# Transposed projections in three 256-column products a step, summed in half a PSUM bank

## The chip, the cores and the metric

The kernel runs on one core of a Trainium2 chip. The metric is the time of one execution on the device, in microseconds (us). TensorE multiplies (PE in the profile; PEld is its load of the stationary operand), VectorE (DVE) and ScalarE (ACT) work on elements, GpSimd (POOL) issues a few transfers, and SyncE (SP) issues the large ones. Products are summed in PSUM, in banks of 512 float32 columns.

## What is computed

Two transformer layers over 256 tokens of width 2048, in float32. Layer 0 has attention with forget gates, layer 1 has sparse attention over keys and values made from layer 0's output. Each layer ends with a squared-Relu MLP of width 8192, and each half of a layer with a layer norm.

```python
def sq_relu_mlp(x, w1, w2):
    return jnp.square(jax.nn.relu(x @ w1)) @ w2
...
    for layer in range(DEPTH):
        if layer < N_A_LAYERS:
            mix = fox_attention(h, fox_w_in[layer], fox_b_f[layer], fox_w_o[layer])
        else:
            b = layer - N_A_LAYERS
            mix = nsa_attention(h, nsa_w_in[b], nsa_w_o[b], rel_bias, *kv)
        h = layer_norm(ALPHA * h + mix, ln1_g[layer], ln1_b[layer])
        h = layer_norm(ALPHA * h + sq_relu_mlp(h, mlp_w1[layer], mlp_w2[layer]), ln2_g[layer], ln2_b[layer])
        if layer == N_A_LAYERS - 1:
            kv = shared_kv(h, kv_w, cmp_pos_k, cmp_pos_v, cmp_k_w1, cmp_k_w2, cmp_v_w1, cmp_v_w2)
```

## The kernel before

Every float32 operand of a large product is held as two parts of type float32r, a high part and a low rest (`fill_split`, L117 on ScalarE for the high part and L118 on VectorE for the rest). A product x @ W is then the sum of three: high by high, high by low, low by high.

Weights come in blocks of 128 partitions x 1024 columns (512 KB), loaded by SyncE's queue into `raw` (4 buffers) and split into `whl` (5 buffers, [128, 2, 1024]: high, low). Activations lie transposed in chunks `act` of [128, 4, 2, 256]: four blocks of 128 features, and for each the high parts of the 256 tokens and, right behind them, the low ones, so that one block gives a contiguous moving operand of 512 columns.

There are two kinds of large product:

- `xs_part` and `xs_mm` (L173) have activations as the stationary operand and 512 columns of weights as the moving one; three 512-column products a step, the first two with the same stationary block. They make values, the output projections and the second matrix of the MLP. The change leaves them alone.
- `ws_many` (L141 to L156) has 128 columns of a matrix, a slice, as the stationary operand and activations as the moving one, so that the product comes out transposed: [128 columns of W, 256 tokens]. A slice is two blocks of weights and 16 steps. A step is a wide product (L151): high weights by the 512 columns of high and low activations, into a whole bank `acc`; and a low product (L152): low weights by the 256 high activations, into the first half of the bank. In the last step the low product comes ahead of the wide one. After 16 steps the two halves of the bank have to be added.

`merge` (L182 to L189) does that: ScalarE copies the second half to SBUF (L185), VectorE adds it to the first half (L187, or L189 with a scale). `ws_many` and `merge` serve the queries and keys of layer 0 (`project`, 32 slices), the hidden layer of both MLPs (`use` in `mlp`, 128 slices; VectorE's L385 then does the squared Relu and `fill_split` fills the next chunk), the transposed keys and values (`use_raw` and `use_k`, 16 slices) and the queries of layer 1 (16 slices). In the attentions the logits, transposes and weighted sums of earlier heads are put between the slices (`at` and `run`). A scheduler sets the order on each engine from the program's order and its own estimates.

In `ws_many` before:

```python
            for w, acc in zip(ws, accs):
                wide = lambda: mm(acc, w[:, 0, s], a, start=kt == 0, stop=last)
                low = lambda: mm(acc[:, :S], w[:, 1, s], a[:, 0, :], start=False, stop=False)
                if last:
                    low(), wide()
                else:
                    wide(), low()
```

Of the kernel before, what the change touches and what calls it, by code (L numbers as in the profile page):

```python
# [19 lines left out]
P = 128  # L20
# [3 lines left out]
G = 4  # L24
# [28 lines left out]
def constants():  # L53
    """Identity, triangles, stacked identities and masks: they depend on shapes alone."""
    i = np.arange(P)
    eye = np.eye(P, dtype=np.float32)
    upper = (i[:, None] <= i[None, :]).astype(np.float32)
    causal = np.where(i[None, :] > i[:, None], np.float32(BIG), np.float32(0))

    def stacked(n):  # L60
        a = np.zeros((P, n), np.float32)
        a[np.arange(2 * n), np.arange(2 * n) % n] = 1
        return a

    t = np.arange(S).reshape(2, P)
    d_c = t[:, :, None] - (16 * np.arange(NC) + 31)
    keep = (d_c >= 0).astype(np.float32).transpose(1, 0, 2).reshape(P, 2 * NC)
    cst = [eye, upper, np.ones((P, P), np.float32), np.zeros((P, P), np.float32), causal,
           stacked(60), stacked(48), stacked(16), keep]

    def onehot(*dists):
        """Block k of 32 rows picks the bucket of distance k; row 96 + k says that the key lies ahead."""
        a = np.zeros((99, len(dists[0])), np.float32)
        c = np.arange(len(dists[0]))
        for k, dist in enumerate(dists):
            ok = dist >= 0
            a[NB * k + buckets(dist)[ok], c[ok]] = -1
            a[96 + k, c[~ok]] = 1
        return a

    oh = [onehot(255 - np.arange(384))]
    for tb in range(2):
        oh += [onehot(*(d_c[tb, :, n + k] for k in range(3))) for n in range(0, NC, 3)]
    ahead = np.zeros((99, 3, H), np.float32)
    ahead[[96, 97, 98], [0, 1, 2]] = BIG
    oh.append(ahead.reshape(99, 3 * H))
    return np.ascontiguousarray(np.concatenate(cst, 1)), np.ascontiguousarray(np.concatenate(oh, 1))
# [11 lines left out]
def _trunk(nc, tc, i, out, ctx):  # L99
# [23 lines left out]
    def wload(src, k, pool=wp, bufs=5, pieces=1):  # L123
        """Half k of a block of weights, split."""
        raw = raw_tile()
# [16 lines left out]
    def ws_many(srcs, acts, accs, half=None):  # L142
        """accs = (128 columns of a matrix each)^T @ x^T, over the wide halves of x; half: rows 0-1023 or the rest."""
        for kt in range(KT) if half is None else range(8 * half, 8 * half + 8):
            if kt % 8 == 0:
                ws = [wload(src, kt // 8) for src in srcs]
            a = acts[kt // 4][:, kt % 4]
            s = slice(kt % 8 * P, (kt % 8 + 1) * P)
            last = kt == KT - 1
            for w, acc in zip(ws, accs):  # L150
                wide = lambda: mm(acc, w[:, 0, s], a, start=kt == 0, stop=last)  # L151
                low = lambda: mm(acc[:, :S], w[:, 1, s], a[:, 0, :], start=False, stop=False)  # L152
                if last:
                    low(), wide()
                else:
                    wide(), low()  # L156

    def ws_stream(srcs, acts, use, together=1):
        """Each of srcs is one 128-column slice of a matrix; use(j, acc) gets its product, transposed."""
        j = 0  # L160
# [14 lines left out]
    def xs_part(src, act, accs, first, last, pieces=1):  # L175
        """accs[t] += (512 columns of x)[tokens t] @ 512 x 512 of a matrix"""
        ws = [wload(src, k, pieces=pieces if k == 0 else 1) for k in range(2)]
# [3 lines left out]

    def merge(dst, acc, scale=1.0):  # L182
        """dst = scale * (the wide product's two halves)"""
        t = sp.tile([P, S], F32, tag="mt", name="mt")
        nc.scalar.activation(t, acc[:, S:], AF.Copy, scale=scale)  # L185
        if scale == 1.0:
            nc.vector.tensor_add(dst, acc[:, :S], t)  # L187
        else:
            nc.vector.scalar_tensor_tensor(dst, acc[:, :S], scale, t, op0=OP.mult, op1=OP.add)  # L189

    def narrow(src, n, acts, st, dst):
        """dst[:, tok, :] = x @ (2048 x n) for a small n; returns its last step."""
        raw = wp.tile([P, KT, n], F32, tag="raw", name="nraw", bufs=4)
# [32 lines left out]
    def out_proj(src, acts, first, ln=None, two=False, between=()):  # L226
        """h = (ALPHA h or h) + acts @ W, 512 columns at a time (two: the first 1024 at once).

        between's steps come after the parts. With ln, the last 512 columns are left to what it returns,
        which ends with the layer norm."""  # L230
        between = list(between)
# [36 lines left out]
        def end(late, meanwhile=None):  # L268
            """Tokens 128-255 come behind, so that the norm of the others overlaps with their products."""
            ln.gains(late)  # L270
# [30 lines left out]
    class Norm:  # L301
        """Layer norm of h in place, in pieces of 128 tokens x 512 features, with what use does to a piece."""

# [55 lines left out]
    def transposer(cs):  # L359
        """Puts the pieces into cs, transposed and split, in chunks of 512 features."""  # L360
        def use(t, c):
# [14 lines left out]
    def mlp(layer, acts, ln):  # L376
        for q in range(4):
            hid = []

            def use(j, acc):  # L380
                if j % 4 == 0:
                    hid.append(act_chunk())
                u = sp.tile([P, S], F32, tag="mu", name="mu")
                merge(u, acc)
                nc.vector.scalar_tensor_tensor(u, u, 0.0, u, op0=OP.max, op1=OP.mult)  # L385
                fill_split(hid[-1][:, j % 4, 0, :], hid[-1][:, j % 4, 1, :], u)
# [5 lines left out]

    # ---- attention: the steps that both kinds share
    def exp_rows(E, L, m, sums):
# [4 lines left out]

    # ================= layer 0: forgetting attention  # L400
    bfb = cp.tile([P, H], F32, name="bfb")
# [8 lines left out]
    def warm(n, lhs, rhs):  # L410
        """Keeps the tensor engine's clock up while it waits."""
        idle = ps_lg.tile([P, 512], F32, tag="lg", name="idle")
# [18 lines left out]
    def forget_gates():  # L431
        """Log of the forget gates."""
        f = sp.tile([P, 5, 2, H], F32, name="f", bufs=1)
# [29 lines left out]
    with tc.tile_pool(name="fp", bufs=2) as fp:  # L463
# [16 lines left out]
        def project(name, hd, sc):  # L480
            acc = acc_tile()
            ws_many([i[name][hd]], xs, [acc])
            x = fp.tile([P, S], F32, tag=name, name=name)
            merge(x, acc, sc)
            return x
# [92 lines left out]
    with tc.tile_pool(name="late", bufs=2) as late:  # L578
# [6 lines left out]
        def tables():  # L585
            """Tables of the relative bias, negated, with BIG where a key lies ahead"""
            r_ps = ps_lg.tile([P, 512], F32, tag="lg", name="rps")
# [17 lines left out]

    # ================= layer 1: sparse attention over keys and values of layer 0's output
    with tc.tile_pool(name="np", bufs=2) as np_:
# [4 lines left out]
        gate = np_.tile([P, 2, 3 * H], F32, name="gate", bufs=1)  # L612
        # keys of the two branches and of the compressed blocks, split: per group, high and low parts of
        # [selected 0-127, window 0-127, compressed, selected 128-255, window 128-255]
        kT = np_.tile([P, G, 2, KW], F32R, name="kT", bufs=1)
        kcT = np_.tile([P, G, NC], F32, name="kcT", bufs=1)
        vhl = np_.tile([P, 2, 2, 512], F32R, name="vhl", bufs=1)
        v1 = np_.tile([P, 2, 512], F32, name="v1", bufs=1)
        # compressed values in three bands of rows (high, high, low parts), to meet high, low and high weights
        vc = np_.tile([BAND, G, P], F32R, name="vc", bufs=1)  # L620
# [5 lines left out]
        def bands(t):  # L626
            """The three bands of the columns of t"""
            return bass.AP(tensor=t.tensor, offset=t.offset, ap=[*[list(x) for x in t.ap[:-1]], [32, 3], [1, NC]])
# [3 lines left out]
        def use_raw(j, acc):  # L632
            merge(raws[:, j // G, j % G, :], acc)

# [20 lines left out]
        def use_k(j, acc):  # L655
            x = np_.tile([P, S], F32, tag="q", name="k")
            merge(x, acc)
            s, g = j // G, j % G
# [16 lines left out]
        def compress(s):  # L675
            """First product of the compression; returns its later steps."""
            acc = acc_tile()
# [158 lines left out]
        for hd in range(H):  # L836
# [7 lines left out]
            qT = np_.tile([P, S], F32, tag="q", name="q")  # L844
            merge(qT, acc, -SCALE)
            at(n + 2, scores(hd, qT, bm))
# [11 lines left out]
def laid_out(a):  # L858
    """The inputs in the order in which the kernel reads them."""
    def cols(w):  # L860
        # 128 columns of all rows, in two halves of the rows: [n, half, p, (kt c)]
        k, n = w.shape
        return w.reshape(2, k // P // 2, P, n // P, P).transpose(3, 0, 2, 1, 4).reshape(n // P, 2, P, HALF)

    def rows(w):
        # 512 columns of 512 rows, in two halves of the rows: [n, kc, half, p, (kt c)]
        k, n = w.shape
# [53 lines left out]
```

## Time and profile before

| what | value |
|---|---|
| median of the runs | 2260.76 us (2259.89 to 2261.65, 3 runs) |
| span of the profiled execution, first to last instruction | 2258.3 us |
| mean granted TensorE clock in it | 0.995 of full speed |
| TensorE's matmuls busy | 2233.2 us (99%) |
| VectorE busy | 1406.5 us (62%) |
| ScalarE busy | 1047.0 us (46%) |
| products of L151, L152 and L173 | 3072, 3072 and 4416 |

The page gives the busy time of an engine as the union of its instructions; matmuls overlap in it, since the next starts streaming before the last has drained. The time line gives starts, and the distance from one start to the next is what a product takes from the engine. The chain of waits goes back from the last instruction to what released it, step by step, and shows what the end of the kernel hung on.

### The profile page before, as it was taken

How to read it: one execution, taken by the hardware profiler on the slowest of the kernel's cores; microseconds unless marked ns; L12 is line 12 of the kernel's file. 1: busy time of each engine (PE TensorE's matmuls, PEld its weight loads, DVE VectorE, ACT ScalarE, POOL GpSimd, SP SyncE). 2: the span in 40 equal slices, each digit the busy share in tenths (PEclk: the TensorE clock that was granted, in tenths of full speed). 3: DMA queues.
4: the chain of work that ended last, by engine and by line, in shares of the span. 5: the costliest groups of instructions: out<-in, count | busy, mean ns of one | idle time of the engine just before them, and what ended most of it. 6: DMA issues, size and time to landing. Idle time of an engine off the chain costs nothing.

```text
span 2258.3 us, 30147 instructions
## 1 busy us (share of the span) xinstructions
PE 2233.2 (99%) x11478; PEld 1890.7 (84%) x11478; DVE 1406.5 (62%) x2209; ACT 1047.0 (46%) x1564; POOL 18.5 (1%) x26
## 2 busy tenths in 40 slices
PE   9999999999999999999999999999999999999997
PEld 7888888888888888888788888888888888888885
DVE  6565556764565565565786688667655645655655
ACT  5444444443444444444355567544434434444442
POOL 0000000000000000000000000000000000000001
PEclk9999999999999999999999999999999999999998
DMA  7665557556555555555556744565565566565563
GB/s 252 197 206 180 173 197 243 195 187 191 191 186 192 192 187 191 191 187 190 183 170 211 252 134 133 171 212 177 187 194 188 187 194 189 186 195 188 187 194 113
DMA packets 116829, 427.54 MB, mean 189 GB/s; under 512 B 13179, under 2 KB 13339, under 8 KB 115406
## 3 DMA queue, kind: packets, MB, share of 16 engines
q1 hardware_dynamic: 114734, 419.00, 56.9%
q0 software_dynamic: 1952, 6.63, 1.0%
q8 instruction: 90, 1.47, 0.3%
q14 instruction: 53, 0.43, 0.1%
HBM read 423.45 MB, written 4.24 MB: 189 GB/s over the span
## 4 chain that ended last, share of the span: by engine, by line
PE 97%; DVE 2%; DMA 1%; ACT 0%; issue 0%; SPq 0%; DVEq 0%
PE acc L173 44%; PE acc L151 31%; PE acc L152 16%; PE acc L683 1%; PE pt L367 1%; PE pt L830 1%; PE pt L808 0%; PE lg L766 0%; DMA bc<-c_dram 0%; DVE h L354 0%; PE acc L199 0%; PE pt L831 0%; PE pt L524 0%; PE lg L491 0%; PE lg L762 0%; DVE h L339 0%
## 5 line engine op out<-in xcount | busy, mean ns | idle before, releaser
L118 DVE TENSOR_TENSOR whl<-raw,whl 128x1024 fp32r<-128x1024 f32 (+1 forms) x769 | 937.9, 1223 | 617.9 <-ACT whl L117 608.5
L117 ACT CAST whl<-raw 128x1024 fp32r<-128x1024 f32 (+1 forms) x769 | 804.5, 1049 | 740.4 <-PE acc L173 489.6
L151 PE MATMUL acc<-act,whl 128*128 128x512 f32 x3072 | 1089.5, 401 | 0.0
L173 PE MATMUL acc<-whl,act 128*128 128x512 f32 x4416 | 1011.7, 390 | 1.0 <-DVE whl L118 1.0
L173 PEld LDWEIGHTS acc<-whl,act 128*128 128x128 f32 x4416 | 827.6, 188 | 175.4 <-DVE whl L118 1.8
L152 PE MATMUL acc<-act,whl 128*128 128x256 f32 x3072 | 834.3, 282 | 0.0
L151 PEld LDWEIGHTS acc<-act,whl 128*128 128x128 f32 x3072 | 569.7, 189 | 124.1 <-issue 0.2
L152 PEld LDWEIGHTS acc<-act,whl 128*128 128x128 f32 x3072 | 581.4, 189 | 16.7
L185 ACT ACTIVATE mt<-acc 128x256 f32<-128x256 f32 x192 | 73.3, 382 | 308.6 <-PE acc L151 308.6
L187 DVE TENSOR_TENSOR mu<-acc,mt 128x256 f32<-128x256 f32 x128 | 54.1, 424 | 120.3 <-ACT mt L185 120.3
L385 DVE SCALAR_TENSOR_TENSOR mu<-mu 128x256 f32<-128x256 f32 x128 | 54.2, 425 | 4.2
L117 ACT CAST act<-mu 128x256 fp32r<-128x256 f32 x128 | 52.0, 408 | 4.3 <-DVE mu L385 2.6
L118 DVE TENSOR_TENSOR act<-mu,act 128x256 fp32r<-128x256 f32 x128 | 53.4, 419 | 0.0
L117 ACT CAST act<-pt 128x256 fp32r<-128x256 f32 x80 | 29.5, 372 | 43.8 <-PE pt L367 32.7
L241 DVE TENSOR_TENSOR h<-h,acc 128x512 f32<-128x512 f32 x48 | 30.8, 681 | 13.2 <-PE acc L173 13.2
L118 DVE TENSOR_TENSOR act<-pt,act 128x256 fp32r<-128x256 f32 x80 | 33.0, 419 | 9.2 <-ACT act L117 9.0
L395 ACT ACTIVATE E<-E,sm 128x128 f32<-128x128 f32 (+1 forms) x64 | 29.0, 453 | 7.7 <-DVE sm L398 7.4
L354 DVE SCALAR_TENSOR_TENSOR h<-h,mv,lnb 128x256 f32<-128x256 f32 (+1 forms) x53 | 26.5, 541 | 0.1
L395 ACT ACTIVATE E<-L,sm 128x128 f32<-128x128 f32 (+1 forms) x32 | 14.3, 449 | 25.3 <-DVE sm L398 25.3
L367 PE MATMUL pt<-cst,h 128*128 128x128 f32 x96 | 18.8, 294 | 6.3 <-DVE h L354 6.0
L339 DVE SCALAR_TENSOR_TENSOR h<-h,mv,lng 128x256 f32<-128x256 f32 (+1 forms) x53 | 25.0, 501 | 0.0
L239 DVE SCALAR_TENSOR_TENSOR h<-h,acc 128x512 f32<-128x512 f32 x32 | 20.6, 680 | 4.5 <-PE acc L173 4.5
(173 smaller groups left out, 664.9 us busy)
## 6 DMA issues: line engine op xcount, KB each, us to landing
raw<-in_w SPq DMA_DIRECT2D x512, 512.0 KB, 3.5
raw<-in_fq SPq DMA_DIRECT2D x32, 512.0 KB, 3.6
raw<-in_fk SPq DMA_DIRECT2D x32, 512.0 KB, 3.5
raw<-in_fo SPq DMA_DIRECT2D x32, 512.0 KB, 3.6
raw<-in_kvT SPq DMA_DIRECT2D x32, 512.0 KB, 4.4
raw<-in_nq SPq DMA_DIRECT2D x32, 512.0 KB, 3.6
raw<-in_no SPq DMA_DIRECT2D x32, 512.0 KB, 3.6
raw<-in_fv SPq DMA_DIRECT2D x31, 512.0 KB, 3.5
```

The source lines that it names most:

```text
L117: nc.scalar.copy(hi, src)
L118: nc.vector.tensor_sub(lo, src, hi.bitcast(F32))
L151: wide = lambda: mm(acc, w[:, 0, s], a, start=kt == 0, stop=last)
L152: low = lambda: mm(acc[:, :S], w[:, 1, s], a[:, 0, :], start=False, stop=False)
L173: mm(acc, l, w[:, r, s], start=first and n == 0, stop=last and n == 2)
L185: nc.scalar.activation(t, acc[:, S:], AF.Copy, scale=scale)
L187: nc.vector.tensor_add(dst, acc[:, :S], t)
L241: nc.vector.tensor_add(hcols(t, n), hcols(t, n), acc)
L354: nc.vector.scalar_tensor_tensor(hs, hs, rstd, b, op0=OP.mult, op1=OP.add)
L367: nc.tensor.transpose(tp[:, k * P:(k + 1) * P], h[:, t, f:f + P], eye)
L385: nc.vector.scalar_tensor_tensor(u, u, 0.0, u, op0=OP.max, op1=OP.mult)
L395: nc.scalar.activation(E, L, AF.Exp, bias=m, scale=-1.0, accum_out=sums)
```

## The change

A step of `ws_many` becomes three products of 256 columns, all summed in the first half of the bank: high weights by high activations, high weights by low activations, low weights by high activations. The second half of the bank isn't used. `merge` goes; `scaled` is one ScalarE copy with a scale from PSUM to its destination. In the MLP ScalarE takes the Relu on the way out of PSUM and VectorE multiplies the result by itself. Comments and docstrings go, so that line numbers move: L151 and L152 become L152 to L154, L173 becomes L171, L385 becomes L378.

```diff
@@ ws_many
             for w, acc in zip(ws, accs):
-                wide = lambda: mm(acc, w[:, 0, s], a, start=kt == 0, stop=last)
-                low = lambda: mm(acc[:, :S], w[:, 1, s], a[:, 0, :], start=False, stop=False)
-                if last:
-                    low(), wide()
-                else:
-                    wide(), low()
+                out = acc[:, :S]
+                mm(out, w[:, 0, s], a[:, 0, :], start=kt == 0, stop=False)
+                mm(out, w[:, 0, s], a[:, 1, :], start=False, stop=False)
+                mm(out, w[:, 1, s], a[:, 0, :], start=False, stop=last)
...
-    def merge(dst, acc, scale=1.0):
-        t = sp.tile([P, S], F32, tag="mt", name="mt")
-        nc.scalar.activation(t, acc[:, S:], AF.Copy, scale=scale)
-        if scale == 1.0:
-            nc.vector.tensor_add(dst, acc[:, :S], t)
-        else:
-            nc.vector.scalar_tensor_tensor(dst, acc[:, :S], scale, t, op0=OP.mult, op1=OP.add)
+    def scaled(dst, acc, scale=1.0):
+        nc.scalar.activation(dst, acc[:, :S], AF.Copy, scale=scale)
...
@@ mlp, use
+                r = sp.tile([P, S], F32, tag="mt", name="mr")
                 u = sp.tile([P, S], F32, tag="mu", name="mu")
-                merge(u, acc)
-                nc.vector.scalar_tensor_tensor(u, u, 0.0, u, op0=OP.max, op1=OP.mult)
+                nc.scalar.activation(r, acc[:, :S], AF.Relu)
+                nc.vector.tensor_mul(u, r, r)
                 fill_split(hid[-1][:, j % 4, 0, :], hid[-1][:, j % 4, 1, :], u)
...
@@ project, use_raw, use_k and the queries of layer 1
-            merge(x, acc, sc)
+            scaled(x, acc, sc)
```

On TensorE, in the MLP of layer 0, the end of one slice and the start of the next stand so before (the number behind a name is the buffer: `acc_5346` is one slice's bank and `acc_5396` the next one's):

```order
L151 MATMUL acc_5346<-act_3275,whl_5369 128x512
L152 MATMUL acc_5346<-act_3275,whl_5369 128x256 x2
L151 MATMUL acc_5346<-act_3275,whl_5369 128x512
L151 MATMUL acc_5396<-act_3272,whl_5398 128x512
L152 MATMUL acc_5396<-act_3272,whl_5398 128x256
```

And so after the change (another slice of the same MLP):

```order
L152 MATMUL acc_6003<-act_3723,whl_6034 128x256
L153 MATMUL acc_6003<-act_3723,whl_6034 128x256
L154 MATMUL acc_6003<-act_3723,whl_6034 128x256
L152 MATMUL acc_6069<-act_3720,whl_6071 128x256
L153 MATMUL acc_6069<-act_3720,whl_6071 128x256
L154 MATMUL acc_6069<-act_3720,whl_6071 128x256
```

Every product has 256 columns now, and a slice ends as its other steps do.

On VectorE, in the same MLP, the rows between two slices' weights before (`mu` is the hidden layer's tile):

```order
L118 TENSOR_TENSOR whl_5570<-raw_5569,whl_5570 128x1024
L187 TENSOR_TENSOR mu_5490<-acc_5447,mt_5491 128x256
L385 SCALAR_TENSOR_TENSOR mu_5490<-mu_5490 128x256
L118 TENSOR_TENSOR whl_5600<-raw_5599,whl_5600 128x1024
L118 TENSOR_TENSOR act_5439<-mu_5490,act_5439 128x256
```

And after (`mr` is ScalarE's Relu):

```order
L118 TENSOR_TENSOR whl_6491<-raw_6490,whl_6491 128x1024
L378 TENSOR_TENSOR mu_6390<-mr_6389 128x256
L118 TENSOR_TENSOR whl_6528<-raw_6527,whl_6528 128x1024
L118 TENSOR_TENSOR act_6323<-mu_6390,act_6323 128x256
L118 TENSOR_TENSOR whl_6533<-raw_6532,whl_6533 128x1024
```

One operation a slice has gone, and the rest keeps its order.

On TensorE, in the attention of layer 1, in the middle of a head's slice (`lg` are logits of one head, `pt` the transposes of the head before it), before:

```order
L762 MATMUL lg_11009<-kT_9048,qhl_11006 128x272 x2
L766 MATMUL lg_11010<-kT_9048,qhl_11006 128x512
L808 MATMUL pt_10986<-cst_80,E_10899 128x128 x3
L809 MATMUL pt_10986<-cst_80,wide0_9053 96x128
L808 MATMUL pt_10996<-cst_80,E_10899 128x128 x3
L809 MATMUL pt_10996<-cst_80,wide0_9053 96x128
L762 MATMUL lg_11009<-kT_9048,qhl_11006 128x272
L766 MATMUL lg_11010<-kT_9048,qhl_11006 128x512 x2
L767 MATMUL lg_11009<-kcT_9049,q_10957 128x15
```

And after, in the same head:

```order
L801 MATMUL pt_12710<-cst_80,E_12609 128x128 x3
L802 MATMUL pt_12710<-cst_80,wide0_10461 96x128
L801 MATMUL pt_12720<-cst_80,E_12609 128x128 x3
L802 MATMUL pt_12720<-cst_80,wide0_10461 96x128
L755 MATMUL lg_12733<-kT_10456,qhl_12730 128x272 x3
L759 MATMUL lg_12734<-kT_10456,qhl_12730 128x512 x3
L760 MATMUL lg_12733<-kcT_10457,q_12675 128x15
```

The transposes stand ahead of the logits; in the other heads they stood there before as well.

## Rows read from the trace of the kernel before

**Rows 1.** The page's first part: engine, busy us, share of the span, instructions.

```profile
PE 2233.2 (99%) x11478; PEld 1890.7 (84%) x11478; DVE 1406.5 (62%) x2209; ACT 1047.0 (46%) x1564; POOL 18.5 (1%) x26
```

**Rows 2.** The page's chain that ended last: share of the span by line.

```profile
PE acc L173 44%; PE acc L151 31%; PE acc L152 16%; PE acc L683 1%; PE pt L367 1%; PE pt L830 1%; PE pt L808 0%; PE lg L766 0%; DMA bc<-c_dram 0%; DVE h L354 0%; PE acc L199 0%; PE pt L831 0%; PE pt L524 0%; PE lg L491 0%; PE lg L762 0%; DVE h L339 0%
```

**Rows 3.** Waits of TensorE: who for whom, us in total, times, longest.

```profile
PE pt L367 <- DVE h L354: 6.0, 6, 2.6
...
PE pt L510 <- DVE E L501: 1.1, 1, 1.1
```

**Rows 4.** Chain of waits, 780 to 850 us: shares, then start us, us, what.

```profile
by line: PE acc L151 66.8%; PE acc L152 33.5%
...
787.38 0.47 PE acc L151 x2
...
843.91 0.47 PE acc L151 x2
```

**Rows 5.** Time line of TensorE, one slice: start us, us, line, operation, tiles.

```profile
803.58 0.28 PE L152 MATMUL acc<-act,whl 128*128 128x256 f32 x1
803.69 0.40 PE L151 MATMUL acc<-act,whl 128*128 128x512 f32 x1
...
804.64 0.28 PE L152 MATMUL acc<-act,whl 128*128 128x256 f32 x1
...
805.70 0.28 PE L152 MATMUL acc<-act,whl 128*128 128x256 f32 x1
```

**Rows 6.** The page's costliest groups: shapes, count, busy us, mean ns, idle before.

```profile
L152 PE MATMUL acc<-act,whl 128*128 128x256 f32 x3072 | 834.3, 282 | 0.0
...
L185 ACT ACTIVATE mt<-acc 128x256 f32<-128x256 f32 x192 | 73.3, 382 | 308.6 <-PE acc L151 308.6
L187 DVE TENSOR_TENSOR mu<-acc,mt 128x256 f32<-128x256 f32 x128 | 54.1, 424 | 120.3 <-ACT mt L185 120.3
L385 DVE SCALAR_TENSOR_TENSOR mu<-mu 128x256 f32<-128x256 f32 x128 | 54.2, 425 | 4.2
```

**Rows 7.** Time line of TensorE at the end of that slice.

```profile
809.59 0.40 PE L152 MATMUL acc<-act,whl 128*128 128x256 f32 x2
809.83 0.63 PE L151 MATMUL acc<-act,whl 128*128 128x512 f32 x2
```

**Rows 8.** Time line of TensorE, weighted sum of a head in layer 1.

```profile
1381.89 0.28 PE L827 MATMUL pt<-pc,vc 96*128 96x256 f32 x1
1382.01 0.53 PE L830 MATMUL pt<-PT,vhl 128*128 128x256 f32 x3
1382.37 0.39 PE L831 MATMUL pt<-PT,v 128*128 128x128 f32 x2
```

**Rows 9.** Chain of waits: two runs of 512-column products.

```profile
855.45 87.05 PE acc L173 x384
...
1174.77 3.73 PE acc L199 x16
```

**Rows 10.** Chain of waits in the first head.

```profile
63.56 0.34 DVE fk L187
...
66.71 0.61 PE pt L510 x3
```

**Rows 11.** Time line of all engines, a head in layer 1: softmax and transposes.

```profile
1303.43 0.35 DVE L794 TENSOR_SCALAR E<-E,sm 128x256 f32<-128x256 f32 x1
...
1304.05 0.49 PE L808 MATMUL pt<-cst,E 128*128 128x128 f32 x3
```

**Rows 12.** A stretch at low clock: stretch, us, engines, clock, DMA; then time line.

```profile
406.00:409.40 3.40, 3.40 (x13) 2.89 (x12) 3.08 (x9) 1.02 (x3) 0.00 (x0) 0.50 1.02 334
...
407.47 0.63 PE L151 MATMUL acc<-act,whl 128*128 128x512 f32 x1
...
408.11 0.63 PE L151 MATMUL acc<-act,whl 128*128 128x512 f32 x1
```

**Rows 13.** Chain of waits: a run of 128-column products.

```profile
1275.55 1.75 PE pt L724 x16
```

More of the change, by code (lines that the diff above doesn't have):

```diff
@@ L632, in use_raw @@
         def use_raw(j, acc):
-            merge(raws[:, j // G, j % G, :], acc)
+            scaled(raws[:, j // G, j % G, :], acc)
         ws_stream([i["kvT"][s, g] for s in range(2) for g in range(G)], xs, use_raw, 3)
@@ L656, in use_k @@
             x = np_.tile([P, S], F32, tag="q", name="k")
-            merge(x, acc)
+            scaled(x, acc)
             s, g = j // G, j % G
@@ L844, in _trunk @@
             qT = np_.tile([P, S], F32, tag="q", name="q")
-            merge(qT, acc, -SCALE)
+            scaled(qT, acc, -SCALE)
             at(n + 2, scores(hd, qT, bm))
```

## Prediction

> **What bounds the kernel now.** I read the page's busy shares first, then its chain of work that ended last, then the chain of waits and the time line inside one slice of a matrix. The reader should see in the first that TensorE's matmuls fill 99% of the span and VectorE and ScalarE 62% and 46% [rows 1], and in the second that nearly all of the chain is TensorE: 44% on the products of L173, 31% on the wide ones of L151 and 16% on the low ones of L152 [rows 2]. TensorE hardly waits for anyone: the longest sums of its idle time are 6.0 us behind the layer norm and 1.1 us behind one softmax [rows 3]. So the time is the number of products times the distance from one product's start to the next one's, and work on VectorE or ScalarE counts only where it ends a wait. A product's own duration (282 ns for 256 columns [rows 6]) is no price, since its neighbours overlap with it; distances between starts are.
>
> In the chain of waits the last wide product of each slice stands with the first of the next. From 787.38 to 843.91 us lie ten slices [rows 4], so a slice takes 5.653 us and each of its 16 steps, one wide and one low product, 353.3 ns. Two thirds of it stand on the wide product and one third on the low one, 66.8 and 33.5% [rows 4]: 235 and 118 ns. Inside a slice three steps take 804.64 to 805.70 us, 1.06 us or again 353.3 ns each [rows 5]. At 2.4 GHz the 768 columns of a step are 320 ns, so 33.3 ns of each step are something else.
>
> **The change part by part. Products.** In 192 slices (128 of the hidden layer, 32 + 16 of queries and keys, 8 + 8 of keys and values) there are 16 steps each, 3072 in all, as the count of L152 says [rows 6]. Each step loses a product of 512 columns and gains two of 256: the same columns, one product and one weight load more. (Loads are not merged now where a stationary block stays, as in L173, whose 4416 products have 4416 loads; I count 9216 of either after the change.) What does a 256-column product cost among its like? Nothing before the change is a long run of them, but there are short ones. At a slice's end two low products stand together: 809.59 to 809.83, 0.24 us for two, 120 ns each [rows 7]. In the sparse attention L827 and three of L830 follow each other, all into the same 256 columns: 1381.89 to 1382.37, 0.48 us for four, 120 ns each [rows 8]. That is 256 / 2.4 + 13.3 ns. The long runs of L173, with a stationary block used twice and then another, as the new triple has it, give 87.05 us / 384 = 226.7 ns, which is 512 / 2.4 and the same 13.3 ns [rows 9]. Three times 120 ns is 360 ns against 353.3: +6.7 ns a step, and 3072 x 6.7 = +20.5 us.
>
> The bounds: after a low product now 118 ns on average; three of those are 354 ns, no change, and below that stands the shortest distance in the slices, 0.11 us from 803.58 to 803.69 [rows 5]. Above, the 16 products of L199, of whole act chunks, run at 3.73 / 16 = 233 ns [rows 9], 20 ns over their columns, and the step's two products now have 16.7 ns each on average; three with 16.7 are 370 ns, +51 us. I take 120, because both runs of 256-column products have it, in act chunks and elsewhere, and because it follows from L173's price.
>
> The Trainium skill's page "TensorE: Matmul & The Clock Gate" has, under "Back-to-back issue gap", N / 2.4 + 2.5 ns between warm matmuls. The trace disagrees: 226.7 where that gives 215.8, and 120 where it gives 109.2. By the Trainium skill's figure the step would go from 325 to 327.5 ns, an estimate of +7.7 us, and the time would be 2267.
>
> **Eviction.** Per slice, ScalarE's copy of the wide half (382 ns) becomes a copy or a Relu of the same size, and VectorE's sum (424 ns) goes [rows 6]. The hidden layer's square on VectorE (425 ns) becomes a product of the same shape; I take the same time, with 382 and 425 as ends, those of the other 256-column operations [rows 6]. VectorE so has 192 x 0.42 = 81 us less work, which is worth nothing where TensorE doesn't wait for it. The wait that may shrink is the first head's: there VectorE's sum of a key (0.34 us of the chain) stands ahead of the softmax whose transposes TensorE waited 1.1 us for [rows 3, 10]; without it, and with the products before it slower, up to 1 us of that wait goes. What is late next is the bias transfer, which doesn't move. I take -1 us, with 0 and -1.1 as ends. The 6.0 us behind the layer norm hang on VectorE's norm steps, which the change leaves alone.
>
> **Order.** In the sparse attention six heads have transposes between the logits' products now; after the change the eight transposes stand first. They read E, which VectorE's L794 finishes at 1303.78 in one head, 0.27 us before the second group of transposes starts at 1304.05 [rows 11]. VectorE has one operation of some 0.4 us less a head in front of it and TensorE some 0.1 us more, so the margin grows and I cost the move at nothing. If that cover were gone, six waits of under 0.3 us make 2 us. The DMA queue keeps its order, and a slice's two loads and splits keep the time of a slice, which grows.
>
> **Clock.** From 406.0 to 409.4 us the granted clock is 0.50, that is 1.2 GHz, after TensorE's idle time at the norm; a step there takes 0.64 us, which is 768 / 1.2, with nothing on top [rows 12]. So the change costs nothing there. A further stretch of 3.4 us at the low level would cost 3.4 x (1 - 353 / 640) = 1.5 us; I allow two either way, 3 us.
>
> **Sum.** 2258.3 us of the profiled span + 20.5 - 1 = 2277.8. The median of the runs lies 2.5 us above that span, so 2280.
>
> **The rivals.** *Cost goes by columns, not by products.* In the present stream both products have a distance of 0.46 ns per column (235 / 512, 118 / 256). If that is what act chunks cost, a triple takes what the step takes now, and only the -1 us is left: 2260. For it: the step's own mean. Against: the pair of low products at 120, out of the same chunks [rows 7], and the evenness of L173 and L830. *The run locks at its shortest distance*: three equal products keep step, as L173's do, but at the 0.11 us that some low products have now. That is rounded to 10 ns; at 0.115 a triple is 345 ns, -25 us, and the time 2234 or below. It decides as soon as the run's distance falls under 117 ns. It is the case on the other side; no row of equal products shows it. *A small constant per product.* At the low clock level a step has nothing on top of its columns [rows 12], and the 13.3 ns could belong to short runs and to whl as the moving side. A constant between 0 and 5 ns, 2.5 in the middle, adds 3072 x 2.5 = +7.7 us: 2267. Against: three runs of different tiles with 13.3. The Trainium skill's formula above would have this result. *16.7 ns on each product*: +51 us, 2311, if the excess of the present mixture goes with act chunks and every product pays it. Against it stands rows 7 again. *TensorE's instructions come too slowly.* A step has six instead of four, one each 60 ns where it was 88. Sixteen products of L724 with their loads ran at 1.75 / 16 = 109 ns, 55 ns an instruction [rows 13], but for 1.75 us only, too short to show a lasting rate. It decides once the lasting price of an instruction passes 60 ns; at 62 a step is 372 ns and the time 2317, at 61 it is 366 and 2298.
>
> That the change doesn't do what it says can be left aside: the order of the changed program has 3072 triples in the place of the pairs.
>
> **How the numbers follow.** What a measurement of this kernel can tell from no change is about 0.2%, 4.5 us. Forecast, 120 ns each, 2272 to 2288 with the clock and the small terms: 0.62. By columns, 2254 to 2264: 0.16, of which 0.03 falls below 2256.2. Shortest distance: 0.04. Small constant: 0.05. 16.7 each: 0.08. Instruction supply: 0.05. So faster 0.07; same 0.15, with 0.02 from the forecast's and the constant's lower tails; slower 0.78. The range 2255 to 2298 holds the forecast, most of the second case, the small constant and the near end of the last: some 0.83.
>
> **What would show it.** Right: slices 5.76 us apart in the hidden layer, products of L152 to L154 each 0.12 us after the one before, L171's runs unchanged at 226.7 ns, VectorE at 59% and TensorE's waits no longer. By columns: slices at 5.65. Instruction supply: distances that start at 120 and grow within a slice. Wrong altogether: a wait for whl or E on TensorE that isn't there now, or distances between 256-column products that differ from place to place.

## The result, and the profile after

The changed kernel takes 2282.57 us (median of 4 runs, 2279.98 to 2282.76) against 2260.34 us before: 1.0093 times the time, with a 95% interval of 1.0078 to 1.0107. That is 22.2 us more, where +20 us, 2280, was forecast.

The page of the changed kernel, its first part and the chain by line, beside [rows 1, 2]: the span is 2281.0 us, TensorE has 3072 products and 3072 loads more, and VectorE is at 58%. The prediction named 59%, but its own terms, (1406.5 - 81) / 2278, give 58.

```profile
span 2281.0 us, 35960 instructions
...
PE 2254.6 (99%) x14550; PEld 2057.2 (90%) x14550; DVE 1332.8 (58%) x2017; ACT 1032.0 (45%) x1564; POOL 18.6 (1%) x26
...
PE acc L171 44%; PE acc L152 16%; PE acc L154 16%; PE acc L153 16%; PE pt L359 1%; PE pt L823 0%; PE lg L759 0%; PE pt L801 0%; DMA bc<-c_dram 0%; PE acc L676 0%; PE acc L191 0%; PE pt L824 0%; PE pt L517 0%; DVE whl L118 0%; PE lg L484 0%; DVE h L346 0%
```

The time line of TensorE inside a slice, beside [rows 5] (start us, us, what). Every product starts 0.12 us after the one before it, without the unevenness of the alternating widths:

```profile
799.96 0.28 PE L152 MATMUL acc<-act,whl 128*128 128x256 f32 x1
800.08 0.28 PE L153 MATMUL acc<-act,whl 128*128 128x256 f32 x1
800.20 0.28 PE L154 MATMUL acc<-act,whl 128*128 128x256 f32 x1
800.32 0.28 PE L152 MATMUL acc<-act,whl 128*128 128x256 f32 x1
...
801.04 0.28 PE L152 MATMUL acc<-act,whl 128*128 128x256 f32 x1
```

Three steps take 799.96 to 801.04 us, 1.08 us or 360 ns each, where it was 353.3.

The cleanest measure of a slice is the stretch between two runs of the MLP's second matrix, which holds 16 slices and nothing else. From the chains of waits, before and then after (start us, us, what):

```profile
500.47 87.05 PE acc L173 x384
677.96 87.05 PE acc L173 x384
```

```profile
508.29 87.07 PE acc L171 x384
687.51 87.07 PE acc L171 x384
```

Before, 677.96 - 500.47 - 87.05 = 90.44 us, 5.653 us a slice; after, 687.51 - 508.29 - 87.07 = 92.15 us, 5.759 us a slice. That is +0.107 us, and 192 times it is 20.5 us. The runs of the untouched 512-column products keep 226.7 ns.

TensorE's waits after, beside [rows 3]:

```profile
PE pt L359 <- DVE h L346: 5.1, 3, 2.6
PE pt L503 <- DVE E L494: 2.4, 1, 2.4
...
PE acc L152 <- ACT act L117: 0.9, 2, 0.5
...
PE acc L152 <- DVE h L346: 0.5, 1, 0.5
```

The wait for the first head's softmax has grown from 1.1 to 2.4 us, where the prediction had it shrink. The waits behind the norms come to 5.1 + 0.9 + 0.5 = 6.5 us, where they were 6.0.

### The profile page after: what moved, and what is told of

Read it like the earlier page. It is cut to its first block, busy times and chain, and to the rows that moved or that the text cites. A ratio compares the mean times of both kernels' runs of the same rounds, so it can differ in the third digit from the quotient of the medians.

```text
span 2281.0 us, 35960 instructions
## 1 busy us (share of the span) xinstructions
PE 2254.6 (99%) x14550; PEld 2057.2 (90%) x14550; DVE 1332.8 (58%) x2017; ACT 1032.0 (45%) x1564; POOL 18.6 (1%) x26
## 4 chain that ended last, share of the span: by engine, by line
PE 96%; DVE 2%; DMA 1%; ACT 0%; issue 0%; SPq 0%; ACTq 0%; DVEq 0%
PE acc L171 44%; PE acc L152 16%; PE acc L154 16%; PE acc L153 16%; PE pt L359 1%; PE pt L823 0%; PE lg L759 0%; PE pt L801 0%; DMA bc<-c_dram 0%; PE acc L676 0%; PE acc L191 0%; PE pt L824 0%; PE pt L517 0%; DVE whl L118 0%; PE lg L484 0%; DVE h L346 0%
## 5 line engine op out<-in xcount | busy, mean ns | idle before, releaser
L171 PE MATMUL acc<-whl,act 128*128 128x512 f32 x4416 | 1011.3, 390 | 1.0 <-ACT whl L117 0.9
L171 PEld LDWEIGHTS acc<-whl,act 128*128 128x128 f32 x4416 | 826.7, 188 | 175.8 <-ACT whl L117 2.8
L152 PE MATMUL acc<-act,whl 128*128 128x256 f32 x3072 | 878.1, 286 | 1.4 <-ACT act L117 0.9
L153 PE MATMUL acc<-act,whl 128*128 128x256 f32 x3072 | 871.3, 284 | 0.0
L154 PE MATMUL acc<-act,whl 128*128 128x256 f32 x3072 | 870.8, 284 | 0.0
L152 PEld LDWEIGHTS acc<-act,whl 128*128 128x128 f32 x3072 | 590.7, 192 | 3.1 <-ACT act L117 2.3
L153 PEld LDWEIGHTS acc<-act,whl 128*128 128x128 f32 x3072 | 590.9, 192 | 1.0 <-issue 0.2
L154 PEld LDWEIGHTS acc<-act,whl 128*128 128x128 f32 x3072 | 590.5, 192 | 0.0
L377 ACT ACTIVATE mr<-acc 128x256 f32<-128x256 f32 x128 | 48.9, 384 | 232.5 <-PE acc L154 232.5
L378 DVE TENSOR_TENSOR mu<-mr 128x256 f32<-128x256 f32 x128 | 54.4, 425 | 126.4 <-ACT mr L377 126.3
L233 DVE TENSOR_TENSOR h<-h,acc 128x512 f32<-128x512 f32 x48 | 30.9, 681 | 13.3 <-PE acc L171 13.3
```

Of the source, the lines that this page charges most:

```text
L152: mm(out, w[:, 0, s], a[:, 0, :], start=kt == 0, stop=False)
L153: mm(out, w[:, 0, s], a[:, 1, :], start=False, stop=False)
L154: mm(out, w[:, 1, s], a[:, 0, :], start=False, stop=last)
L171: mm(acc, l, w[:, r, s], start=first and n == 0, stop=last and n == 2)
L233: nc.vector.tensor_add(hcols(t, n), hcols(t, n), acc)
L377: nc.scalar.activation(r, acc[:, :S], AF.Relu)
```

## The experiments

The theory: what a step costs is set by the number and width of its products, 13.3 ns each over its columns where the width stays, and in the old step some more for the alternation. The rivals are in the expectations. Each version is compared with the kernel before on the same chip, which took 2259.06 us beside the first four versions and 2260.38 us beside the last four.

**Products alone.** Three products in 14 of 16 steps, but into both halves of the bank, with the old merge:

```diff
@@ ws_many of the kernel before
-                wide = lambda: mm(acc, w[:, 0, s], a, start=kt == 0, stop=last)
                 low = lambda: mm(acc[:, :S], w[:, 1, s], a[:, 0, :], start=False, stop=False)
-                if last:
-                    low(), wide()
-                else:
-                    wide(), low()
+                if last:
+                    low()
+                if kt == 0 or last:
+                    mm(acc, w[:, 0, s], a, start=kt == 0, stop=last)
+                else:
+                    mm(acc[:, :S], w[:, 0, s], a[:, 0, :], start=False, stop=False)
+                    mm(acc[:, S:], w[:, 0, s], a[:, 1, :], start=False, stop=False)
+                if not last:
+                    low()
```

> One part alone: three 256-column products a step in 14 of 16 steps (first and last step as before), but high by low into the second half of the bank, with the merge kept as before. Theory: the count of products makes the difference; 2688 steps x 6.7 ns = +18 us, 2278 us, and the eviction's 81 us of VectorE work less are worth about nothing. Rival: the slowdown comes from summing all three into one half bank, or from the new eviction; then 2260 us.

Measured: 2278.87 us, a ratio of 1.0083 (1.0069 to 1.0097). Between two runs of the second matrix, 16 slices take 684.69 - 505.99 - 87.06 = 91.64 us, 1.20 us more than before, or 14.4 us over the 192 slices:

```profile
505.99 87.06 PE acc L177 x384
684.69 87.06 PE acc L177 x384
```

The expectation had 18 us, because it left the two steps with a wide product at the price of the alternation. But the wide product that ends a slice stands next to the one that starts the next slice, and little alternation is left: at the prices of equal widths a slice is 44 x 120 + 2 x 226.7 ns = 5.733 us, and 5.728 were measured. The profiled span is 17.6 us longer than before (2275.9 against 2258.3). Besides the 14.4, TensorE waits 1.0 us longer for the first softmax (2.1 us), and the granted clock is 0.50, that is 1.2 GHz, behind the second norm too (from 1136.6 to 1140.0 us), which the prediction prices at 1.5 us.

So the products make the slice longer without the shared half bank and without the new eviction, at the 120 ns that they cost in the changed kernel, although neighbours write to different halves of the bank here. The 81 us less on VectorE are worth nothing that can be measured.

**Another order of the three products.** With high by high, low by high, high by low, no stationary block stands twice in a row:

```diff
@@ ws_many of the changed kernel
                 mm(out, w[:, 0, s], a[:, 0, :], start=kt == 0, stop=False)
-                mm(out, w[:, 0, s], a[:, 1, :], start=False, stop=False)
-                mm(out, w[:, 1, s], a[:, 0, :], start=False, stop=last)
+                mm(out, w[:, 1, s], a[:, 0, :], start=False, stop=False)
+                mm(out, w[:, 0, s], a[:, 1, :], start=False, stop=last)
```

> The changed kernel with the products of a step in the order high by high, low by high, high by low, so that no stationary block stands twice in a row. Theory: every product loads its own block in any case, 120 ns each, and the time is that of the changed kernel, 2282 us within 0.2%. Rival: a repeated stationary block is cheaper; then this order is slower, by as much as the load takes (up to some ns a step; 2 ns a step would be 6 us, 2288 us).

Measured: 2282.22 us, ratio 1.0098 (1.0083 to 1.0114). The chain of waits of this version has the same stretch of 16 slices, 688.05 - 508.83 - 87.07 = 92.15 us:

```profile
508.83 87.07 PE acc L171 x384
688.05 87.07 PE acc L171 x384
```

A repeated stationary block is not cheaper.

**All products with 512 columns.** The low product runs over the low activations too:

```diff
@@ ws_many of the kernel before
-                wide = lambda: mm(acc, w[:, 0, s], a, start=kt == 0, stop=last)
-                low = lambda: mm(acc[:, :S], w[:, 1, s], a[:, 0, :], start=False, stop=False)
-                if last:
-                    low(), wide()
-                else:
-                    wide(), low()
+                mm(acc, w[:, 0, s], a, start=kt == 0, stop=False)
+                mm(acc, w[:, 1, s], a, start=False, stop=last)
```

> The kernel before with the low product over all 512 columns (low by low is added, which the reference has in its float32 products and the kernel before leaves out): both products of a step have 512 columns. Theory of a constant and a price of alternation: no alternation is left, two products of 226.7 ns, a step of 453.3 ns, 3072 x 100 ns = +307 us, 2568 us. Rival, that 512 columns of an activation chunk cost 233 ns: a step of 466.7 ns, +348 us, 2609 us.

Measured: 2571.29 us in one run, 3 us above the theory's 2568. Two runs of the second matrix stand 781.98 - 578.89 - 87.04 = 116.05 us apart, 453.3 ns a step, to the last digit of the theory:

```profile
578.89 87.04 PE acc L169 x384
781.98 87.04 PE acc L169 x384
```

So activation chunks as the moving operand cost no more than weights do, and the 235 ns of the wide product in the kernel before belong to the alternation with a narrower one. L199's 233 ns [rows 9] were a poor guide; its stationary blocks have 96 columns there (32 in its other use), and why it pays more stays open.

**Runs of one width.** If alternation costs 6.7 ns a step, the kernel before can be made faster by putting equal widths together: eight wide products of a block of weights, then its eight low ones, in the second block the other way round, so that runs of sixteen arise:

```diff
@@ ws_many of the kernel before, in place of its loop
+        for hb in range(2) if half is None else (half,):
+            ws = [wload(src, hb) for src in srcs]
+            kts = range(8 * hb, 8 * hb + 8)
...
+            def wides(w, acc):
+                for kt in kts:
+                    s = slice(kt % 8 * P, (kt % 8 + 1) * P)
+                    mm(acc, w[:, 0, s], acts[kt // 4][:, kt % 4], start=kt == 0, stop=kt == KT - 1)
...
+            def lows(w, acc):
+                for kt in kts:
+                    s = slice(kt % 8 * P, (kt % 8 + 1) * P)
+                    mm(acc[:, :S], w[:, 1, s], acts[kt // 4][:, kt % 4, 0, :], start=False, stop=False)
...
+            for w, acc in zip(ws, accs):
+                for f in ((wides, lows) if hb == 0 else (lows, wides)):
+                    f(w, acc)
```

> The kernel before with its products in another order: of each block of weights eight wide products in a row and then eight low ones (in the second block the low ones first), nothing else changed. Theory: a product costs its columns at 2.4 GHz and 13.3 ns, and the alternation of wide and low costs another 6.7 ns a step; then a step is 226.7 + 120 = 346.7 ns in place of 353.3, and the time 2260 - 3072 x 6.7 ns = 2240 us. Rival: the wide product of activation chunks costs 233 ns wherever it stands (as L199's sixteen do); then a step stays at 353 ns and the time at 2260 us.

Measured: 2250.09 us, ratio 0.9957 (0.9944 to 0.9969): faster than both kernels, but 9 us instead of 20. The time line of TensorE in a slice of the hidden layer:

```profile
782.11 3.82 PE L151 MATMUL acc<-act,whl 128*128 128x512 f32 x16
785.77 2.08 PE L156 MATMUL acc<-act,whl 128*128 128x256 f32 x16
787.68 1.55 PE L151 MATMUL acc<-act,whl 128*128 128x512 f32 x6
```

Sixteen wide products take 785.77 - 782.11 = 3.66 us, 228.8 ns each, and sixteen low ones 1.91 us, 119.4 ns each. The wide ones don't reach 226.7 on average. I had taken the price for one of the single change; the next run shows that it lasts longer. That is the smaller part of what is missing. In the MLPs 16 slices take 674.81 - 498.70 - 87.04 = 89.07 us where they took 90.44, which is 11.0 us for the 128 slices of the hidden layers, and 6.7 ns a step would have made 13.7:

```profile
498.70 87.04 PE acc L177 x384
674.81 87.04 PE acc L177 x384
```

The span fell by 9.3 us (2258.3 to 2249.0), so everything outside these slices, with the 64 slices of the attentions, lost 1.7 us where the theory had a gain of 6.9. There the runs of wide products are mostly eight long, and logits and transposes break them. The version also has a stretch at 0.50, the low level (1.2 GHz), behind the second norm, where the kernel before has none; the prediction prices one at 1.5 us. The rest of the loss was not traced. Stretch, us, engines, clock, DMA, of this version, then of the kernel before:

```profile
1121.50:1124.80 3.30, 3.30 (x9) 2.52 (x9) 3.10 (x9) 0.86 (x3) 0.00 (x0) 0.50 0.00 0
```

```profile
1125.40:1128.80 3.40, 2.96 (x17) 2.12 (x16) 3.31 (x10) 1.09 (x4) 0.00 (x0) 1.00 0.00 0
```

**Runs of four.** The same with four and four (in the last four rows of a slice low ahead of wide):

```diff
@@ ws_many of the version above
-            kts = range(8 * hb, 8 * hb + 8)
+            for q in (8 * hb, 8 * hb + 4):
+                kts = range(q, q + 4)
...
-                for f in ((wides, lows) if hb == 0 else (lows, wides)):
+                    for f in ((lows, wides) if q == 12 else (wides, lows)):
```

> The kernel before with four wide products in a row, then four low ones, and so on. Theory, from the trace of the version with runs of sixteen: after a change of width the first wide products take 234, 236, 228 and 232 ns and the first low ones 113, 119, 120 and 120, and only then 226.7 and 120; the price hangs on the change. Then four steps are 930 + 472 = 1402 ns, 350.5 ns each, between the 353.3 of the alternation and the 347.9 of runs of sixteen; a slice of the hidden layer takes 5.61 us and the time is 2251 to 2258 us. Rival: the price belongs to the first product of a run alone; then four steps are 3 x 346.7 + 353.3, 348.3 ns each, a slice of 5.57 us.

Measured: 2252.38 us in one run. The time line of TensorE in a slice:

```profile
602.02 2.00 PE L152 MATMUL acc<-act,whl 128*128 128x512 f32 x8
603.86 0.64 PE L157 MATMUL acc<-act,whl 128*128 128x256 f32 x4
604.33 1.09 PE L152 MATMUL acc<-act,whl 128*128 128x512 f32 x4
605.26 0.63 PE L157 MATMUL acc<-act,whl 128*128 128x256 f32 x4
605.73 1.09 PE L152 MATMUL acc<-act,whl 128*128 128x512 f32 x4
606.66 1.12 PE L157 MATMUL acc<-act,whl 128*128 128x256 f32 x8
607.62 2.00 PE L152 MATMUL acc<-act,whl 128*128 128x512 f32 x8
```

From 602.02 to 607.62 us is a slice, 5.60 us, where the theory had 5.61 and its rival 5.57. Wide products in a run of four take 0.93 / 4 = 232 ns, in a run of eight 1.84 / 8 = 230, in sixteen 228.8, without a change of width 226.7, and one by one 235. The price of a change is spread over several wide products behind it, and the low ones give back little: 118 ns in fours, 120 in eights.

**Four products a step.** The low by high product of the changed kernel in two of 128 columns, which stand between the other two products:

```diff
@@ ws_many of the changed kernel
                 mm(out, w[:, 0, s], a[:, 0, :], start=kt == 0, stop=False)
-                mm(out, w[:, 0, s], a[:, 1, :], start=False, stop=False)
-                mm(out, w[:, 1, s], a[:, 0, :], start=False, stop=last)
+                for k in range(0, S, P):
+                    mm(acc[:, k:k + P], w[:, 1, s], a[:, 0, k:k + P], start=False, stop=False)
+                mm(out, w[:, 0, s], a[:, 1, :], start=False, stop=last)
```

> The changed kernel with the low by high product of each step split into two of 128 columns. Theory: a product has its own weight load, and below some width the load sets the distance, 109 ns as in the transposes; a step is 120 + 109 + 109 + 120 = 458 ns, +98 x 3072 = +301 us, 2583 us. Rival: columns and 13.3 ns hold at 128 columns too, 66.7 ns each; a step of 373 ns, +41 us, 2323 us.

Measured: 2602.51 us in one run, where the theory had 2583 and its rival 2323; a step takes (791.89 - 586.22 - 87.06) / 256 = 0.4633 us:

```profile
586.22 87.06 PE acc L172 x384
791.89 87.06 PE acc L172 x384
```

That is +103 ns on the changed kernel's step where the load's floor gave +98 and the constant alone +13. So 13.3 ns over the columns is no law for narrow products: four products with four loads need 116 ns each on average, and the same columns in narrower pieces cost 320 us. That it is the loads that set this distance is not shown. In the time line the starts within a step are not the expected 120, 109, 109 and 120:

```profile
676.35 0.28 PE L152 MATMUL acc<-act,whl 128*128 128x256 f32 x1
676.47 0.34 PE L154 MATMUL acc<-act,whl 128*128 128x128 f32 x2
676.65 0.33 PE L155 MATMUL acc<-act,whl 128*128 128x256 f32 x1
676.82 0.28 PE L152 MATMUL acc<-act,whl 128*128 128x256 f32 x1
```

The two narrow ones stand close together, 0.18 us for both, and the product behind them takes 0.17 us until the next one starts. The sum comes within 5 ns of the theory's 458, the single distances don't fit it.

**The first heads' softmax, a slice later.** In the changed kernel and in the version with runs of sixteen:

```diff
-                later = 3 if hg == 0 else 2
+                later = 4 if hg == 0 else 2
```

> The changed kernel with the first four heads' softmax one step (one slice) later. Theory: of the changed kernel's 22 us, about 1.3 are a longer wait of TensorE for the first head's softmax (2.4 us against 1.1), behind the transfers of the gate sums; with a slice more in between the wait is gone and the time falls by some 2.4 us, to 2280 us. Rival: the wait only moves to the next step that needs the same data; then the time stays at 2282 us.

> The kernel before with eight wide and eight low products in a row and with the first four heads' softmax one slice later. Theory: the gain of the grouping (9.5 us against the kernel before) and of the wait of 1.4 us add up, 2259 - 11 = 2248 us. Rival: the later softmax only moves a wait; then 2250 us. The two are close to what five rounds can tell.

Measured: 2280.96 us in one run of the first. The wait for E is gone from TensorE's list, and the span is 2279.2 us against 2281.0:

```profile
PE pt L359 <- DVE h L346: 5.1, 3, 2.6
PE idle L407 <- DVE blank L410: 1.5, 1, 1.5
PE acc L171 <- ACT whl L117: 1.0, 1, 1.0
PE acc L171 <- DVE whl L118: 1.0, 2, 0.8
```

That speaks for the theory, but 1.8 us of one profile and 1.6 us of one run are close to the noise. The second took 2251.08 us, ratio 0.9957 (0.9944 to 0.9971), no better than without, which is the time that the rival gives. The rival's reason isn't shown, though. The wait for E is gone here too, and TensorE waits 1.1 us for the gate sums' input instead, a wait that the version without the edit doesn't list:

```profile
PE pt L456 <- DVE lf L452: 1.1, 1, 1.1
```

In the chain of waits these products (L456) stand ahead of the softmax's transposes (L514), so the later softmax didn't push that wait along, and why it comes stays open:

```profile
43.78 0.40 PE pt L456 x2
72.79 0.33 PE pt L514 x3
```

## Why the prediction was right, point by point

**What bounds the kernel.** Right: the chain is TensorE's before and after, and the count and width of its products account for nearly all of the change. VectorE's relief was worth nothing that can be seen: products and waits of TensorE make up the difference in the changed kernel and in the version with the old merge.

**The price of a product.** Right to the digit of the trace: 120 ns for each 256-column product, 360 ns a step, 5.759 us a slice (5.76 was named). The two short rows of equal products in the trace of before, two low products at a slice's end [rows 7] and four products of a weighted sum [rows 8], were the rows to go by. The prediction took the difference of two measured steps and left 33.3 ns of the old one without a cause. The experiments give it: two products of 13.3 ns over their columns, and 6.7 ns for the alternation. The change adds 13.3 ns with its third product and takes the 6.7 away. The upper bound from L199 was too high by the whole distance to 226.7; the version with 512 columns throughout shows that.

**The rivals.** That cost goes by columns fell with 92.15 us for 16 slices. That the run locks at its shortest distance fell with the even 0.12 us. Nor did instructions come too slowly: 60 ns each held over whole slices, and the version with four products a step has eight in 463 ns, 58 ns each. The case of a small constant stands refuted by the same 92.15 us: the step grew by 6.7 ns and not by 2.5. That rival's sum also left out that two such products make 325 ns, 28 less than the old step. The Trainium skill's gap of N / 2.4 + 2.5 ns ("TensorE: Matmul & The Clock Gate", "Back-to-back issue gap"), which that section gives for an isolated matmul, is the distance in none of these streams; 226.7 and 120 ns are measured over thousands of products.

**The small terms.** Here one step failed. The softmax's wait was to give back 1 us, and it cost 1.3 more (2.4 against 1.1 us). The chain of waits in the first head, of which [rows 10] are the end, shows where, before and then after: the transfer of the gate sums took 2 us longer, and the bias transfer behind it started 2.1 us later.

```profile
44.44 2.68 DMA c_dram<-cr
47.42 5.55 DMA bc<-c_dram
```

```profile
44.58 4.68 DMA c_dram<-cr
49.55 5.27 DMA bc<-c_dram
```

I had written that the bias transfer doesn't move, and that was the step that failed. In the profiles of four other versions the transfer of the gate sums takes 3.2 to 4.8 us, and the wait goes with it: 1.3 and 1.4 us where the transfer takes 3.2 and 3.5, 2.1 to 2.6 us where it takes 4.7 to 4.8, and 2.1 with the old merge too. So the short transfer of the kernel before may be the exception; what sets its length wasn't tried further. The VectorE operation that was removed ahead of the softmax (0.34 us [rows 10]) is gone from the chain, and too small to matter beside the transfer.

**The clock.** One low stretch has moved, as the allowance for it supposed. After the second norm the changed kernel has 0.50 where the kernel before had none, and after the third one it has 1.00 where the kernel before had 0.50 (1.2 GHz; [rows 12] show the first norm's). Stretch, us, engines, clock, DMA, of the changed kernel, then of the kernel before:

```profile
1139.70:1143.10 3.40, 3.40 (x17) 3.40 (x17) 2.55 (x8) 1.02 (x3) 0.00 (x0) 0.50 0.00 0
1545.00:1548.40 3.40, 2.94 (x22) 2.51 (x23) 3.10 (x9) 1.02 (x3) 0.00 (x0) 1.00 0.00 0
```

```profile
1529.00:1532.40 3.40, 3.40 (x12) 2.81 (x12) 3.13 (x10) 1.02 (x3) 0.00 (x0) 0.50 0.00 0
```

They weigh against each other. That the change costs nothing at the low level holds as well: in the first of these stretches three products take 1142.29 to 1142.93 us, 0.64 us, as the old step did [rows 12].

```profile
1142.29 0.41 PE L152 MATMUL acc<-act,whl 128*128 128x256 f32 x1
...
1142.93 0.37 PE L152 MATMUL acc<-act,whl 128*128 128x256 f32 x1
```

Of the 22.7 us between the two spans, 20.5 are the products and 1.3 the first head; 0.9 us are left, 0.5 of it behind the norms, and that is less than the runs scatter.

**The order.** The transposes put ahead of the logits in layer 1 caused no wait: no line of that head's transposes is in TensorE's list after.

## What to carry to other kernels

Where TensorE's chain is the time, count products and loads, and price them by the distance between starts in a row of their own kind; here a pair and a row of four, read to 10 ns, gave the price of thousands. There was luck in it: L199's row was 6 ns off, and the first products behind a change of width differ from the later ones. The same columns in more products cost more here (360 ns a step in three, 463 in four), and relief on an engine that nobody waited for paid for none of it. Putting products of one width together gained 0.43% here without any other edit.

## What the runs showed of the hardware that I had not expected

- A change of width has a price that fades: wide products one by one between low ones take 235 ns, in fours 232, in eights 230, in sixteens 228.8, without a change 226.7. What in TensorE does this was not found.
- A stream of products of one width with 128-column stationary blocks goes at an even step: 120 ns for 256 columns, 226.7 for 512, whether weights or activations move (at 512) and whether a stationary block repeats or not (at 256). That is 13.3 ns over the columns at 2.4 GHz; at the low level the 13.3 ns are not there, three products of 256 columns take 0.64 us.
- Two 128-column products in the middle of 256-column ones start close together, and the next ones pay: 463 ns for the four products of a step, 116 each on average.
